# Two decoder layers in fp32 on one core: more 2x2 blocks with seven products in the feed-forward, and masked decay logs on ScalarE

## The chip, the core and the metric

The kernel runs on one core of a Trainium2 chip. The metric is the device time of one execution in microseconds (us), the median of several runs. Engines are named as the profile names them: PE is TensorE (PEld its weight loads), DVE VectorE, ACT ScalarE, POOL GpSimd, SP SyncE, whose queue issues the weight transfers.

## What is computed

Two layers over 256 tokens of width 2048, everything in fp32. Cut to what matters here:

```python
h = rms_norm(x, norm_mix_w[l])
proj = h @ w_in                                   # 2048 x about 6360 columns
y = concat([retention(...), mamba2(...), rwkv7(...)])
x = x + y @ w_out[l]
h = rms_norm(x, norm_ffn_w[l])
x = x + (silu(h @ ffn_w_gate[l]) * (h @ ffn_w_up[l])) @ ffn_w_down[l]   # D_FF = 5632
# in mamba2, for each of 16 heads and each chunk of 128 tokens:
a_cum = cumsum(dt * A); seg = a_cum[:, None] - a_cum[None, :]
decay_in = exp(where(causal, seg, -inf))          # 128 x 128 a head and chunk
```

## The kernel before

**One product in three passes.** Each fp32 operand is split into two fp32r tiles, high and low (x = xh + xl, w = wh + wl), and a product is xh·wh + xl·wh + xh·wl: three matmuls into one PSUM bank. 256 tokens are two row tiles (t = 0, 1) of 128. The weights are split on the chip: `fetch` has SP load raw tiles of 128x1024 (512 KB, five buffers `raw`), `split` lets ACT write `wh` (a copy to fp32r) and DVE `wl` (raw minus wh), with three buffers each. `plan` writes down the whole sequence of weight tiles ("parts"); `wtile` hands out the next part and emits the split of the one after it. The tiles' framework reorders instructions from this order by priority, but each engine then works through a fixed list.

**Gate and up.** `gate_up` makes 512 columns of gate and 512 of up at once (11 groups f a layer). Its inner dimension runs over eight pairs kp of two k-tiles. A pair is a product of 2x2 blocks: rows t, inner k, columns n (gate or up). Plain pairs take 8 block products, that is 24 matmuls. Pairs in `SEVEN` take 7 (21 matmuls) by a Winograd-like scheme: four PSUM banks C (`dn`) take what belongs to one output alone, four banks M (`mx`) what several share. Such a pair needs sums of weight blocks made on the chip: from two raw tiles DVE makes u1 (128x1024) and u2 (two ops of 128x512), then three tiles are split instead of two, and half a tile b besides. The parts are called s0, s1, s2. The sums of x blocks (`comb`) are made once a layer in `post_pair`, on POOL. After the last such pair ACT and DVE make z, w and y out of the banks M, and at the end of the group they add the banks C, take silu and multiply. `finish` (queued in `self.late`, run in the next group) transposes the result for the down projection and splits it.

**Down.** D_FF is done in two parts of 6 and 5 groups. For each of four column groups g `dense` multiplies over 12 or 10 pairs with two PSUM banks, 12 matmuls a raw tile, and `add_res` adds them to the residual `res`. Of four banks `dn` two are in use at a time. After the last part `post_x` transposes the new residual for the next layer.

**Mixers.** While the input projection runs in `dense`, generators in lanes (`queue`, `pump`) slip the mixers' small steps between its matmuls. `ssm_dt` has `masked` make the causal decay logs: for 8 heads at once, tril times a (high and low part apart), 128x1024 by one POOL op. There are 16 such ops in all, 8 a layer. Two matmuls with `triu_r` sum them, ACT takes exp. Not far from there in time, `rwkv`'s group norm runs on DVE as TENSOR_SCALAR of 128x64 a head (L113).

Of the kernel before, what the change touches and what calls it, by code (L numbers as in the profile page):

```python
# [23 lines left out]

FFN_PARTS = [6, 5]

SEVEN = (2, 5)

# [29 lines left out]
class Trunk:  # L58
# [194 lines left out]
    def plan(self):  # L253
        seq, parts, done = [], [], []

        def plain(tiles, kind="n"):
            for t in tiles:
                parts.append((kind, len(seq)))
                seq.append(t)
                done.append(len(seq))  # L260
        for l in range(DEPTH):
            off = 0
            for n in (IN_W[name] for name in IN_ORDER):
                plain((f"win{l}", off + kp * 2 * P * n, n) for kp in range(8))
                off += D * n
            for g in range(4):
                plain(("wout", (l * 4 + g) * D * 512 + kp * 2 * P * 512, 512) for kp in range(8))
            f0 = 0
            for nf in FFN_PARTS:
                for f in range(f0, f0 + nf):  # L270
                    for kp in range(8):
                        t = [("wgu", ((l * 11 + f) * 16 + 2 * kp + j) * P * 1024, 512) for j in range(2)]
                        if kp in SEVEN:
                            parts += [(f"s{j}", len(seq)) for j in range(3)]
                            seq += t
                            done += [len(seq)] * 3
                        else:
                            plain(t, "c")
# [145 lines left out]
    def post_pair(self, kp, src, scale, xh, xl):  # L424

        fl = lambda t: t.rearrange("p a b -> p (a b)")
        ps = self.PS()
        for k in range(2):
            for t in range(2):
                self.tr(ps[:, k * 256 + t * P:k * 256 + (t + 1) * P], src(t, k), self.ident)  # L430
        w = self.U()
        for k in range(2):
            self.act(w[:, k * 256:(k + 1) * 256], ps[:, k * 256:(k + 1) * 256], AF.Copy, scale=scale(k))
        self.act(fl(xh), w[:, :512], AF.Copy)
        self.tt(fl(xl), w[:, :512], fl(xh).bitcast(F32), ALU.subtract)
        if kp in SEVEN:
            a11, a21, a12, a22, s1, s2, s3, q = [w[:, i * P:(i + 1) * P] for i in range(8)]
            self.tt(s1, a21, a22, ALU.subtract, eng="pool")
            self.tt(s2, s1, a11, ALU.subtract, eng="pool")
            self.tt(s3, a11, a21, ALU.subtract, eng="pool")  # L440
            self.tt(q, a12, s2, ALU.add, eng="pool")
            c = self.U(F32R)
            self.act(c[:, 0:512], w[:, 512:1024], AF.Copy)
            self.tt(c[:, 512:1024], w[:, 512:1024], c[:, 0:512].bitcast(F32), ALU.subtract)
            self.comb[kp] = c
# [549 lines left out]
    def ssm_dt(self, l, raw):  # L995
# [58 lines left out]
        tl = self.cst("tril").rearrange("p (o c) -> p o c", o=1).to_broadcast([P, 8, P])  # L1054
# [12 lines left out]
        y = M["y"] = [None, None]  # L1067
# [217 lines left out]
        self.finish_x()  # L1285
        self.yt = None

    def gate_up(self, rstd):

        mm = self.nc.tensor.matmul  # L1290

# [6 lines left out]
        for kp in range(8):  # L1298
            xk = [self.xs(2 * kp + j) for j in range(2)]
            A = lambda t, k: tuple(h[:, t * P:(t + 1) * P] for h in xk[k])  # L1300
            if kp not in SEVEN:
                for k in range(2):
                    w = self.wtile(("c",))
                    for t in range(2):
                        for n in range(2):
                            prod(C[2 * t + n], A(t, k), blk(w, n), kp == 0 and k == 0, kp == 7 and k == 1)
            else:
                cb = self.comb[kp]
                S1, S2, S3, Q = [(cb[:, i * P:(i + 1) * P], cb[:, 512 + i * P:512 + (i + 1) * P]) for i in range(4)]
                first, last = kp == SEVEN[0], kp == SEVEN[-1]  # L1310
# [12 lines left out]
            if kp == 0:  # L1323
                self.flush()
            if kp == SEVEN[-1]:
                t0, t1, sg = self.U(), self.U(), self.U()
                z, w_, y, v = t0[:, 0:512], t0[:, 512:1024], t1[:, 0:512], t1[:, 512:1024]
                c0, c1 = sg[:, 0:512], sg[:, 512:1024]
                self.act(v, M[0], AF.Copy)
                self.tt(z, v, M[3], ALU.add)  # L1330
                self.tt(w_, M[1], z, ALU.subtract)
                self.tt(y, M[2], z, ALU.add)
# [11 lines left out]
        def finish(t):  # L1344
# [3 lines left out]
            o, p4 = hh[:, :, t * P:(t + 1) * P], ps.rearrange("p (k c) -> p k c", k=4)  # L1348
            self.act(o, p4, AF.Copy)
            self.tt(hl[:, :, t * P:(t + 1) * P], p4, o.bitcast(F32), ALU.subtract)  # L1350
        self.late += [lambda: finish(0), lambda: finish(1)]
        return hh, hl

    def ffn(self, l):
        f0 = 0
        xt, rstd = self.xt, self.rstd
        for pi, nf in enumerate(FFN_PARTS):
            hts = [self.gate_up(rstd) for f in range(f0, f0 + nf)]
            lastp = pi == len(FFN_PARTS) - 1

            def xs(k):
# [4 lines left out]
            for g in range(4):
                kps = list(range(2 * f0, 2 * (f0 + nf)))
                if lastp and l + 1 == DEPTH:
                    if g == 0:
                        fw = self.final_weight()  # L1370
                    if g == 3:
                        return self.final(kps, xs, fw)
                ps = self.dense(512, kps, xs, False)
                self.add_res(g, ps)
                if lastp:
                    if l + 1 < DEPTH:
                        self.post_x(l + 1, g, "nmw")
                    else:
                        self.squares(g)
                        for t in range(2):  # L1380
                            r = self.res[g][:, t, :]
                            self.tt(r, r, fw(g), ALU.mult)
# [122 lines left out]
def _layout(i):  # L1505
# [65 lines left out]

# [20 lines left out]
```

## Time and profile before

| | |
|---|---|
| median of 3 runs | 2423.09 us (2422.21 to 2423.18) |
| profiled execution | 2423.65 us, its span 2421.6 us |
| mean granted PE clock | 0.996 |
| HBM read | 430.66 MB, 179 GB/s over the span |

The span runs from the first instruction to the last; the time has some 2 us around it. Busy times and shares count one engine over the span. A group's line names the helper that records it: L103 is any DVE `tt`, L106 any POOL one, L121 any `act`, L307 and L308 the halves of a weight tile, L1294 a product in `gate_up`, L390 to L392 one in `dense`. In the tables by stretch, a column gives busy us and, in brackets, how many instructions.

### The profile page before, as it was taken

The page shows a single profiled execution, that of the slowest core. Times are in us where ns is not written, and L with a number is a line of the kernel's source. Part 1 is how long each engine was busy: PE and PEld are TensorE (multiplying, and loading weights), DVE is VectorE, ACT ScalarE, POOL GpSimd, SP SyncE. Part 2 cuts the span into 40 slices and gives each one's busy share as a digit, 9 for nine tenths or more (in the row PEclk, how much of TensorE's full clock was granted, in tenths as well). Part 3 has the DMA queues.
Part 4 walks back from the last instruction along what each step waited for, and adds up shares of the span by engine and source line. Part 5 has one row for each costly group of instructions (what it writes and reads, how often), then busy time and mean ns, then how long its engine had stood idle before and what let it go on. Part 6 is the DMA issues. An engine that isn't in the chain of part 4 may idle for free. (4 is left out here: it accounts for less than half of the span.)

```text
span 2421.6 us, 33651 instructions
## 1 busy us (share of the span) xinstructions
PE 2389.3 (99%) x13076; PEld 2023.5 (84%) x13076; DVE 1675.4 (69%) x2106; ACT 1206.7 (50%) x1506; POOL 152.1 (6%) x157
## 2 busy tenths in 40 slices
PE   8999899999999999999999999999999999999998
PEld 8998788888888878888899988887888888888886
DVE  7777756577886467876558876565878754688754
ACT  6445545555554345554454546455555543455543
POOL 2100320000000000000001113200000000000000
PEclk9999999999999999999999999999999999999999
DMA  8454345556555555565544544445555655555654
GB/s 290 147 170 115 133 154 174 179 184 202 192 197 190 189 188 194 187 213 191 184 164 143 165 122 153 157 165 182 192 195 188 200 191 191 184 197 196 215 187 144
DMA packets 139424, 436.01 MB, mean 180 GB/s; under 512 B 30464, under 2 KB 30720, under 8 KB 139264
## 3 DMA queue, kind: packets, MB, share of 16 engines
q1 hardware_dynamic: 137360, 428.52, 53.4%
q0 software_dynamic: 1184, 4.19, 0.5%
q8 instruction: 102, 1.67, 0.3%
q10 hardware_dynamic: 720, 1.15, 0.1%
q14 instruction: 58, 0.48, 0.1%
HBM read 430.66 MB, written 3.15 MB: 179 GB/s over the span
## 5 line engine op out<-in xcount | busy, mean ns | idle before, releaser
L308 DVE TENSOR_TENSOR wl<-raw,wh 128x1024 fp32r<-128x1024 f32 (+3 forms) x763 | 928.0, 1218 | 494.2 <-ACT wh L307 487.2
L307 ACT ACTIVATE wh<-raw 128x1024 fp32r<-128x1024 f32 (+3 forms) x763 | 793.8, 1042 | 893.1 <-PE dn L391 443.4
L1294 PE MATMUL dn<-wh,xh 128*128 128x512 f32 x1100 | 431.4, 392 | 2.3 <-DVE res L103 2.3
L1294 PE MATMUL dn<-wl,xh 128*128 128x512 f32 x1100 | 428.6, 390 | 0.0
L1294 PE MATMUL dn<-wh,xl 128*128 128x512 f32 x1100 | 428.5, 390 | 0.0
L391 PE MATMUL dn<-wh,u 128*128 128x512 f32 x920 | 363.4, 395 | 0.0
L390 PE MATMUL dn<-wh,u 128*128 128x512 f32 x920 | 363.0, 395 | 0.0
L392 PE MATMUL dn<-wl,u 128*128 128x512 f32 x920 | 362.1, 394 | 0.3 <-DVE wl L308 0.2
L382 PE MATMUL dn<-xh,wh 128*128 128x256 f32 x896 | 258.8, 289 | 7.8 <-ACT wh L307 7.8
L384 PE MATMUL dn<-xh,wl 128*128 128x256 f32 x896 | 254.8, 286 | 1.1 <-DVE wl L308 1.1
L383 PE MATMUL dn<-xl,wh 128*128 128x256 f32 x896 | 255.1, 285 | 0.0
L1294 PEld LDWEIGHTS dn<-wh,xh 128*128 128x128 f32 x1100 | 206.5, 188 | 48.9 <-DVE u L103 3.9
L1294 PEld LDWEIGHTS dn<-wl,xh 128*128 128x128 f32 x1100 | 206.4, 188 | 43.4
L1294 PEld LDWEIGHTS dn<-wh,xl 128*128 128x128 f32 x1100 | 206.6, 188 | 42.1
L390 PEld LDWEIGHTS dn<-wh,u 128*128 128x128 f32 x920 | 172.8, 188 | 40.3 <-DVE u L103 0.8
L392 PEld LDWEIGHTS dn<-wl,u 128*128 128x128 f32 x920 | 172.9, 188 | 39.8 <-DVE wl L308 1.1
L391 PEld LDWEIGHTS dn<-wh,u 128*128 128x128 f32 x920 | 172.8, 188 | 38.7
L382 PEld LDWEIGHTS dn<-xh,wh 128*128 128x128 f32 x896 | 173.7, 194 | 10.5 <-ACT wh L307 8.2
L392 PE MATMUL dn<-wl,xh 128*128 128x512 f32 (+2 forms) x448 | 164.3, 368 | 11.0 <-DVE wl L308 11.0
L384 PEld LDWEIGHTS dn<-xh,wl 128*128 128x128 f32 x896 | 173.1, 194 | 1.8 <-DVE wl L308 1.5
L383 PEld LDWEIGHTS dn<-xl,wh 128*128 128x128 f32 x896 | 173.9, 194 | 0.2
L390 PE MATMUL dn<-wh,xh 128*128 128x512 f32 (+2 forms) x448 | 170.9, 382 | 0.0
(177 smaller groups left out, 2725.6 us busy)
## 6 DMA issues: line engine op xcount, KB each, us to landing
raw<-wgu SPq DMA_DIRECT2D x352, 512.0 KB, 3.8
raw<-wdown SPq DMA_DIRECT2D x176, 512.0 KB, 4.2
raw<-win SPq DMA_DIRECT2D x175, 512.0 KB, 3.5
raw<-wout SPq DMA_DIRECT2D x64, 512.0 KB, 3.3
raw<-win SPq DMA_DIRECT2D x32, 340.0 KB, 2.9
raw<-win SPq DMA_DIRECT2D x16, 360.0 KB, 3.0
u<-xt SPq DMA_DIRECT2D x8, 256.0 KB, 7.2
res<-x SPq DMA_DIRECT2D x4, 512.0 KB, 5.2
```

Source lines behind the costliest of these rows:

```text
L307: nc.scalar.activation(wh[:, c], raw[:, c], AF.Copy)
L308: nc.vector.tensor_tensor(wl[:, c], raw[:, c], wh[:, c].bitcast(F32), op=ALU.subtract)
L382: nc.tensor.matmul(o, lhsT=wh[:, c], rhs=xh, start=st and m % 2 == 0, stop=False)
L383: nc.tensor.matmul(o, lhsT=wh[:, c], rhs=xl, start=False, stop=False)
L384: nc.tensor.matmul(o, lhsT=wl[:, c], rhs=xh, start=False, stop=sp and m % 2 == 1)
L390: nc.tensor.matmul(o, lhsT=xh[:, x], rhs=wh[:, c], start=st, stop=False)
L391: nc.tensor.matmul(o, lhsT=xl[:, x], rhs=wh[:, c], start=False, stop=False)
L392: nc.tensor.matmul(o, lhsT=xh[:, x], rhs=wl[:, c], start=False, stop=sp)
L1294: mm(o, lhsT=x[a], rhs=w[b], start=start and i == 0, stop=stop and i == 2)
```

## The change

1. `SEVEN` goes from two pairs to three of eight: kp = 2, 4, 5. Pairs 4 and 5 follow each other.
2. The inner loop of `gate_up` becomes `blocks`, and the down projection uses it too (`down`): two column groups at once as the two block columns, with seven products in pairs 2, 5, 8, 14, 17 and 19 of 22. The weights lie accordingly in `wdp`. The last two column groups of the last part of layer 2 stay in `dense` and `final`. So 21 pairs of the down projection have seven products: 6 in each of the first three of the parts, 3 in the last.
3. The sums of blocks of the hidden activations (`hcomb`) that this needs are made in `finish`, on DVE (`block_sums`), for one pair in six of the eleven groups of a layer.
4. `masked` makes its logs head by head on ACT, copy with a scale per partition: 128x128 each, 64 a layer in the place of 8 POOL ops.

Both versions compute the same function. The diff, without the layout of the weights on the host:

```diff
-SEVEN = (2, 5)
+SEVEN = (2, 4, 5)
+DOWN_SEVEN = (2, 5, 8, 14, 17, 19)
...
-                for g in range(4):
-                    plain(("wdown", (l * 4 + g) * D_FF * 512 + kp * 2 * P * 512, 512)
-                          for kp in range(2 * f0, 2 * (f0 + nf)))
+                    pairs("wgu", (l * 11 + f) * 16, range(8), SEVEN)
+                lastp = f0 + nf == 11
+                for g2 in range(2):
+                    if lastp and l + 1 == DEPTH and g2:
+                        for g in range(2):
+                            plain(("wdown", g * 2 * nf * 2 * P * 512 + kp * 2 * P * 512, 512) for kp in range(2 * nf))
+                    else:
+                        pairs("wdp", (l * 2 + g2) * 44, range(2 * f0, 2 * (f0 + nf)), DOWN_SEVEN)
...
+    def block_sums(self, w, eng):
+        eng = None if eng == "dve" else eng
+        a11, a21, a12, a22, s1, s2, s3, q = [w[:, i * P:(i + 1) * P] for i in range(8)]
+        self.tt(s1, a21, a22, ALU.subtract, eng=eng)
+        self.tt(s2, s1, a11, ALU.subtract, eng=eng)
+        self.tt(s3, a11, a21, ALU.subtract, eng=eng)
+        self.tt(q, a12, s2, ALU.add, eng=eng)
+        c = self.U(F32R)
+        self.act(c[:, 0:512], w[:, 512:1024], AF.Copy)
+        self.tt(c[:, 512:1024], w[:, 512:1024], c[:, 0:512].bitcast(F32), ALU.subtract)
+        return c
...
         def masked(i):
             r = []
             for ap in (ah.bitcast(F32), al):
                 m = self.U(F32R)
-                self.tt(m[:, :1024].rearrange("p (h c) -> p h c", h=8), tl,
-                        ap[:, 8 * i:8 * i + 8].rearrange("p (h o) -> p h o", o=1).to_broadcast([P, 8, P]),
-                        ALU.mult, eng="pool")
+                for h in range(8):
+                    self.act(m[:, h * P:(h + 1) * P], tl, AF.Copy, scale=ap[:, 8 * i + h:8 * i + h + 1])
+                    if h % 4 == 3:
+                        yield 1
                 r.append(m)
-                yield 2
...
-    def gate_up(self, rstd):
+    def blocks(self, kps, xs, comb, mid):
...
-            if kp == SEVEN[-1]:
-                t0, t1, sg = self.U(), self.U(), self.U()
...
+                if last:
+                    mid(M)
...
+            for b in need:
+                self.act(need[b][:, 0:512].rearrange("p (k s c) -> p k s c", k=2, s=2)[:, :, t, :],
+                         p4[:, 2 * b:2 * b + 2, :], AF.Copy)
+                if t:
+                    self.hcomb[2 * f + b] = self.block_sums(need[b], "dve")
+        need = {b: self.U() for b in range(2) if 2 * f + b in DOWN_SEVEN}
         self.late += [lambda: finish(0), lambda: finish(1)]
...
+    def down(self, g2, kps, xs):
+        t0, t1 = self.U(), self.U()
+        z, w, y, v = t0[:, 0:512], t0[:, 512:1024], t1[:, 0:512], t1[:, 512:1024]
+        r = [self.res[2 * g2 + n][:, t, :] for t in range(2) for n in range(2)]
+        def mid(M):
+            self.sums_of(M, v, z, w, y)
+            self.tt(r[0], r[0], v, ALU.add)
+            self.tt(v, M[1], y, ALU.subtract)
+            for a, b in ((1, w), (2, y), (3, v)):
+                self.tt(r[a], r[a], b, ALU.add)
+        C, _ = self.blocks(kps, xs, self.hcomb, mid)
+        for a in range(4):
+            self.tt(r[a], r[a], C[a], ALU.add)
```

Here is how the fixed lists change at three places. First DVE in the third gate and up group of layer 1, from the second split of pair 3 on. In the list before come the splits of pair 4 and then pair 5; `wl` is a half of a weight tile, L329 is u1, L331 and L332 are u2, L336 is b:

```order
L308 TENSOR_TENSOR wl_5778<-raw_5664,wh_5777 128x1024
L308 TENSOR_TENSOR wl_5796<-raw_5696,wh_5795 128x1024
L329 TENSOR_TENSOR u_5831<-raw_5724,raw_5769 128x1024
L331 TENSOR_TENSOR u_5832<-u_5831,raw_5724 128x512
L308 TENSOR_TENSOR wl_5814<-raw_5722,wh_5813 128x1024
L332 TENSOR_TENSOR u_5832<-u_5832,raw_5769 128x512
L336 TENSOR_TENSOR u_5840<-raw_5769,u_5840 128x512
L308 TENSOR_TENSOR wl_5837<-raw_5724,wh_5836 128x1024
L308 TENSOR_TENSOR wl_5860<-u_5831,wh_5859 128x1024
L308 TENSOR_TENSOR wl_5873<-u_5832,wh_5872 128x1024
```

In the changed list (L317 is the half of a tile there, L338, L340, L341 and L345 the sums), DVE at the same place:

```order
L317 TENSOR_TENSOR wl_5872<-raw_5749,wh_5871 128x1024
L338 TENSOR_TENSOR u_5889<-raw_5790,raw_5816 128x1024
L317 TENSOR_TENSOR wl_5895<-raw_5790,wh_5894 128x1024
L340 TENSOR_TENSOR u_5890<-u_5889,raw_5790 128x512
L317 TENSOR_TENSOR wl_5918<-u_5889,wh_5917 128x1024
L341 TENSOR_TENSOR u_5890<-u_5890,raw_5816 128x512
L345 TENSOR_TENSOR u_5898<-raw_5816,u_5898 128x512
L338 TENSOR_TENSOR u_5940<-raw_5818,raw_5863 128x1024
L317 TENSOR_TENSOR wl_5931<-u_5890,wh_5930 128x1024
L340 TENSOR_TENSOR u_5941<-u_5940,raw_5818 128x512
L317 TENSOR_TENSOR wl_5946<-raw_5818,wh_5945 128x1024
L341 TENSOR_TENSOR u_5941<-u_5941,raw_5863 128x512
```

Two runs of sums now interlock, with no plain pair between them.

Second, POOL in the mixers of layer 1, from the rsqrt of `rwkv`'s group norm on (a power of 128x8). Before, six masks (`u<-cc,ah` and `u<-cc,s`, 128x1024) come behind it:

```order
L106 TENSOR_TENSOR s_3164<-s_3164,negh 128x8
L106 TENSOR_TENSOR u_3234<-cc,ah_2981 128x1024
L106 TENSOR_TENSOR u_3269<-cc,s_2983 128x1024
L106 TENSOR_TENSOR u_3310<-cc,ah_2981 128x1024
L106 TENSOR_TENSOR u_3334<-cc,s_2983 128x1024
L106 TENSOR_TENSOR u_3450<-cc,ah_2981 128x1024
L106 TENSOR_TENSOR u_3470<-cc,s_2983 128x1024
L106 TENSOR_TENSOR u_3560<-u_3542,cc 128x4x64 x2
```

Now POOL goes from the power to the rotary ops of retention:

```order
L108 TENSOR_TENSOR u_3156<-u_3078,s_3036 128x1024
L108 TENSOR_TENSOR s_3164<-s_3164,negh 128x8
L108 TENSOR_TENSOR u_3597<-u_3579,cc 128x4x64 x4
L108 TENSOR_TENSOR u_3811<-u_3793,cc 128x4x64 x4
L108 TENSOR_TENSOR u_2359<-u_2359,u_3873 128x512
```

Third, ACT at the same time, in the last columns z of the input projection (weight tiles of 128x680). Before:

```order
L307 ACTIVATE wh_3257<-raw_3110 128x680
L307 ACTIVATE wh_3278<-raw_3148 128x680
L121 ACTIVATE u_3242<-mx_3243,pp_79 128x256 x2
L121 ACTIVATE u_3242<-mx_3250,pp_79 128x256 x2
L307 ACTIVATE wh_3298<-raw_3175 128x680
L307 ACTIVATE wh_3322<-raw_3193 128x680
L121 ACTIVATE u_3318<-u_3242 128x1024
L307 ACTIVATE wh_3342<-raw_3226 128x1024
```

And changed, with the masks (`u<-cc,ah` and `u<-cc,s`, 128x128) between the weight tiles:

```order
L316 ACTIVATE wh_3260<-raw_3110 128x680
L123 ACTIVATE u_3234<-cc,ah_2981 128x128 x4
L316 ACTIVATE wh_3283<-raw_3148 128x680
L123 ACTIVATE u_3245<-mx_3246,pp_79 128x256 x2
L123 ACTIVATE u_3245<-mx_3253,pp_79 128x256 x2
L123 ACTIVATE u_3295<-cc,s_2983 128x128 x4
L316 ACTIVATE wh_3307<-raw_3175 128x680
L123 ACTIVATE u_3295<-cc,s_2983 128x128 x4
L123 ACTIVATE u_3329<-u_3245 128x1024
L316 ACTIVATE wh_3333<-raw_3193 128x680
```

The weight tiles of the input projection now stand behind four masks each in ACT's list.

More of the change, by code (lines that the diff above doesn't have):

```diff
@@ L260, in plain, with pairs @@
                 done.append(len(seq))
+        def pairs(w, first, kps, seven):
+            for kp in kps:
+                t = [(w, (first + 2 * kp + j) * P * 1024, 512) for j in range(2)]
+                if kp in seven:
+                    parts.extend((f"s{j}", len(seq)) for j in range(3))
+                    seq.extend(t)
+                    done.extend([len(seq)] * 3)
+                else:
+                    plain(t, "c")
         for l in range(DEPTH):
@@ L270, in plan @@
                 for f in range(f0, f0 + nf):
[L271 to L278, printed above, removed]
-                for g in range(4):
-                    plain(("wdown", (l * 4 + g) * D_FF * 512 + kp * 2 * P * 512, 512)
-                          for kp in range(2 * f0, 2 * (f0 + nf)))
+                    pairs("wgu", (l * 11 + f) * 16, range(8), SEVEN)
[4 more added lines that the diff above has]
+                            plain(("wdown", g * 2 * nf * 2 * P * 512 + kp * 2 * P * 512, 512) for kp in range(2 * nf))
+                    else:
+                        pairs("wdp", (l * 2 + g2) * 44, range(2 * f0, 2 * (f0 + nf)), DOWN_SEVEN)
                 f0 += nf
@@ L436, in post_pair @@
         if kp in SEVEN:
[L437 to L445, printed above, removed]
+            self.comb[kp] = self.block_sums(w, "pool")
+    def block_sums(self, w, eng):
[9 more added lines that the diff above has]
+        return c
     def squares(self, g):
@@ L1297, in gate_up @@
         blk = lambda w, j: tuple(t[:, j * 512:(j + 1) * 512] for t in w)
-        for kp in range(8):
-            xk = [self.xs(2 * kp + j) for j in range(2)]
+        seven = [kp for kp in kps if kp in comb]
+        for kp in kps:
+            xk = [xs(2 * kp + j) for j in range(2)]
             A = lambda t, k: tuple(h[:, t * P:(t + 1) * P] for h in xk[k])
-            if kp not in SEVEN:
+            if kp not in seven:
                 for k in range(2):
@@ L1305, in gate_up @@
                         for n in range(2):
-                            prod(C[2 * t + n], A(t, k), blk(w, n), kp == 0 and k == 0, kp == 7 and k == 1)
+                            prod(C[2 * t + n], A(t, k), blk(w, n), kp == kps[0] and k == 0, kp == kps[-1] and k == 1)
             else:
-                cb = self.comb[kp]
+                cb = comb[kp]
                 S1, S2, S3, Q = [(cb[:, i * P:(i + 1) * P], cb[:, 512 + i * P:512 + (i + 1) * P]) for i in range(4)]
-                first, last = kp == SEVEN[0], kp == SEVEN[-1]
+                first, last = kp == seven[0], kp == seven[-1]
                 if first:
@@ L1357, in ffn @@
         for pi, nf in enumerate(FFN_PARTS):
-            hts = [self.gate_up(rstd) for f in range(f0, f0 + nf)]
+            self.hcomb = {}
+            hts = [self.gate_up(f, rstd) for f in range(f0, f0 + nf)]
             lastp = pi == len(FFN_PARTS) - 1
@@ L1365, in ffn, with mid, last_group @@
                 self.new_x()
[L1366 to L1376, printed above, removed]
-                        self.post_x(l + 1, g, "nmw")
[L1378 to L1382, printed above, removed]
-            f0 += nf
+            kps = list(range(2 * f0, 2 * (f0 + nf)))
+            for g2 in range(2):
+                last = lastp and l + 1 == DEPTH
+                if last and g2:
+                    ps = self.dense(512, kps, xs, False)
+                    self.add_res(2, ps)
+                    self.last_group(2, fw)
+                    return self.final(kps, xs, fw)
+                if last:
+                    fw = self.final_weight()
+                self.down(g2, kps, xs)
+                for g in (2 * g2, 2 * g2 + 1):
+                    if last:
+                        self.last_group(g, fw)
+                    elif lastp:
+                        self.post_x(l + 1, g, "nmw")
+            f0 += nf
+    def down(self, g2, kps, xs):
+        t0, t1 = self.U(), self.U()
+        z, w, y, v = t0[:, 0:512], t0[:, 512:1024], t1[:, 0:512], t1[:, 512:1024]
+        r = [self.res[2 * g2 + n][:, t, :] for t in range(2) for n in range(2)]
+        def mid(M):
+            self.sums_of(M, v, z, w, y)
[6 more added lines that the diff above has]
+            self.tt(r[a], r[a], C[a], ALU.add)
+    def last_group(self, g, fw):
+        self.squares(g)
+        for t in range(2):
+            r = self.res[g][:, t, :]
+            self.tt(r, r, fw(g), ALU.mult)
     def final_weight(self):
@@ L1488, in _tiles, with _pairs @@
     return np.ascontiguousarray(w.reshape(k, 2, P, n).transpose(0, 2, 1, 3)).reshape(-1)
-def _pairs(a, b):
+def _pairs(a, b, seven):
     k = a.shape[0] // (2 * P)
@@ L1496, in _pairs @@
     for kp in range(k):
-        if kp in SEVEN:
+        if kp in seven:
             o[kp, 0, :, 0], o[kp, 0, :, 1], o[kp, 1, :, 0], o[kp, 1, :, 1] = \
```

33 lines of the change are left out of this document (21 added, 12 removed).

## The prediction

> **What bounds the kernel now.** I read the engine shares on the page first, then what PE waited for, then stretches of the feed-forward.
>
> ```profile
> PE 2389.3 (99%) x13076; PEld 2023.5 (84%) x13076; DVE 1675.4 (69%) x2106; ACT 1206.7 (50%) x1506; POOL 152.1 (6%) x157
> ```
>
> In the list of waits (total us, times, longest), the first three of PE are:
>
> ```profile
> PE dn L392 <- DVE wl L308: 11.2, 5, 6.0
> PE dn L382 <- ACT wh L307: 7.8, 3, 6.0
> PE dn L1294 <- DVE res L103: 2.3, 2, 1.5
> ```
>
> PE hardly waits: 21.3 us in these three, of which the 7.8 fall in the first 250 us and stay. The time is the number of matmuls times their distance, plus a few stalls. The busy 0.39 us of a row overlaps its neighbours; the price of a matmul is the distance of starts. In PE's timeline these two rows of gate and up are 24 matmuls apart, and so are the two of the down projection:
>
> ```profile
> 523.03 0.39 PE L1294 MATMUL dn<-wh,xl 128*128 128x512 f32 x1
> ...
> 528.47 0.39 PE L1294 MATMUL dn<-wh,xl 128*128 128x512 f32 x1
> ```
> ```profile
> 789.84 0.40 PE L390 MATMUL dn<-wh,u 128*128 128x512 f32 x1
> ...
> 795.41 0.39 PE L390 MATMUL dn<-wh,u 128*128 128x512 f32 x1
> ```
>
> That is 5.44/24 = 0.227 us and 5.57/24 = 0.232 us. Three gate and up groups by stretch (us, then PE, PEld, DVE, ACT, POOL busy, clock, DMA share, GB/s):
>
> ```profile
> 531.50:574.30 42.80, 42.80 (x193) 35.21 (x192) 34.41 (x39) 22.60 (x25) 0.00 (x0) 1.00 0.58 193
> ...
> sum 128.60, PE 128.60 PEld 105.78 DVE 103.30 ACT 68.19 POOL 0.00; mean PE 42.87 PEld 35.26 DVE 34.43 ACT 22.73 POOL 0.00
> ```
>
> PE is full, and DVE is the next engine, at 34.4 of 42.9 us. That is what the change loads further.
>
> **Products.** A seven-product pair has 21 matmuls instead of 24. Gate and up: 22 groups x 3 = 66, x 0.227 = 15.0 us. Down: 21 pairs x 3 = 63, x 0.232 = 14.6 us. All lie on the bounding engine: **-29.6 us**.
>
> **Masks.** Where POOL makes masks, DVE stands still. POOL, DVE and PE in their timelines:
>
> ```profile
> 260.52 1.89 POOL L106 TENSOR_TENSOR u<-cc,ah 128x1024 fp32r<-128x1024 f32 x1
> ...
> 269.78 2.52 POOL L106 TENSOR_TENSOR u<-cc,s 128x1024 fp32r<-128x1024 f32 x1
> ```
> ```profile
> 260.58 7.44 DVE L113 TENSOR_SCALAR u<-u,s,s 128x64 f32<-128x64 f32 x4 [1.75 <-POOL s L106]
> 267.94 2.60 DVE L308 TENSOR_TENSOR wl<-raw,wh 128x680 fp32r<-128x680 f32 x1
> 270.47 2.55 DVE L113 TENSOR_SCALAR u<-u,s,s 128x64 f32<-128x64 f32 x4
> 278.39 0.87 DVE L308 TENSOR_TENSOR wl<-raw,wh 128x680 fp32r<-128x680 f32 x1 [0.51 <-ACT wh L307]
> ```
> ```profile
> 270.60 0.65 PE L392 MATMUL dn<-wl,xh 128*128 128x340 f32 x1 [6.02 <-DVE wl L308]
> ```
>
> Four tiny group-norm ops take 7.44 us, one POOL mask each, and the half of a weight tile behind them 2.60 us instead of 0.87. PE waits 6.0 us, and then its granted clock is down:
>
> ```profile
> 265.00:270.00 5.00, 0.00 (x0) 0.00 (x0) 5.00 (x3) 0.00 (x0) 5.00 (x4) 0.93 0.00 0
> 270.00:275.00 5.00, 4.40 (x17) 4.35 (x18) 5.00 (x8) 1.08 (x2) 2.30 (x1) 0.50 0.28 85
> 275.00:280.00 5.00, 5.00 (x31) 5.00 (x30) 3.18 (x4) 2.97 (x6) 0.00 (x0) 0.89 0.81 295
> ```
>
> At half clock for 4.4 us and 0.89 for 5 us PE loses 2.2 + 0.5 = 2.7 us more. PE's waits at the masks further on in layer 1, and in layer 2, with one stretch there:
>
> ```profile
> PE dn L392 <- DVE wl L308: 1.2, 1, 1.2
> ...
> PE dn L392 <- DVE wl L308: 3.8, 2, 2.5
> ```
> ```profile
> 1480.00:1485.00 5.00, 2.61 (x15) 2.09 (x14) 5.00 (x6) 4.49 (x7) 3.41 (x2) 1.00 0.04 16
> ```
>
> Together 6.0 + 2.7 + 1.2 + 3.8 = 13.7 us hang on these ops. They leave POOL, so DVE is free there. SBUF — State Buffer in the Trainium skill ("Who interferes with whom") says that DVE and GpSimd take one shared port pair for a whole instruction, and that ScalarE never waits for it; the 1.86 us that each blocked op takes agree, and by that rule alone the whole 13.7 us would come back and the sum below be 2 us lower.
>
> What comes instead is load on ACT. A copy with a scale per partition of 128x128 isn't in the trace; two rows bracket it:
>
> ```profile
> L121 ACT ACTIVATE s<-dn,s 128x16 f32<-128x16 f32 x4 | 1.1, 275 | 0.8 <-PE dn L392 0.8
> L121 ACT ACTIVATE u<-dn,s 128x340 f32<-128x340 f32 x8 | 4.3, 540 | 2.3 <-PE dn L392 2.3
> ```
>
> Between them, 128 columns are 275 + 112/324 x 265 = 367 ns, so 64 are at most 23 us a layer, in some 60 us of the input projection. ACT is 50% busy over the span, so on the whole it fits. At one spot in each layer it crowds: from one 128x680 tile to the next ACT now has four masks and four 128x256 copies, some 3 us, while PE uses up such a tile in about 1.8 (12 x 0.227 x 340/512) and has two in hand. I give back 1 us a layer. The ends are nothing gained (ACT is late by as much as DVE was) and 13.7; I take the near end because the blocked rows are many times their free length: **-11.7 us**.
>
> **Ends of groups.** The 2.3 us of PE on `res` are the two turns from `dense` to gate and up, where two banks close only at the end. In `down` the first bank closes 9 matmuls (2 us) before the end and its add takes 0.7, so they go. Against that, `post_x` of two column groups now comes at once at the end of layer 1, 8 pieces of 128x256 on DVE behind four adds: between 0 and 5 us, what these pieces take (8 x 0.6, bounded by a 128x512 op); I take 2, since the next projection starts with other columns. **-0.3 us.**
>
> **DVE in gate and up.** Prices, by line and form, and the true distance of DVE's starts:
>
> ```profile
> L308 DVE TENSOR_TENSOR wl<-raw,wh 128x1024 fp32r<-128x1024 f32 x713 | 875.5, 1230 | 477.2 <-ACT wh L307 470.5
> L329 DVE TENSOR_TENSOR u<-raw,raw 128x1024 f32<-128x1024 f32 x44 | 53.6, 1219 | 11.8 <-DMA raw<-wgu 11.6
> L331 DVE TENSOR_TENSOR u<-u,raw 128x512 f32<-128x512 f32 x44 | 30.4, 691 | 1.4
> L103 DVE TENSOR_TENSOR u<-u,u 128x128 f32<-128x128 f32 x4 | 1.1, 284 | 0.0
> ```
> ```profile
> 747.27 1.22 DVE L308 TENSOR_TENSOR wl<-raw,wh 128x1024 fp32r<-128x1024 f32 x1
> 748.41 0.68 DVE L103 TENSOR_TENSOR u<-u,dn 128x512 f32<-128x512 f32 x1
> 749.00 0.68 DVE L103 TENSOR_TENSOR u<-mx,u 128x512 f32<-128x512 f32 x1
> ```
>
> So 1.14 us for 128x1024 and 0.6 for 128x512. A plain pair costs DVE 2 x 1.14 = 2.3 us against 5.4 of PE; a seven-product pair 4 x 1.14 + 3 x 0.6 + 0.1 = 6.5 us against 21 x 0.227 = 4.8. A group goes from 34.4 to 38.6 us, and with block sums for the down projection (4 x 0.28 + 0.6 = 1.7) to 40.3, of 42.2 us of PE. On average it holds; in the burst of pairs 4 and 5 it doesn't, and DVE lives on its lead. The lead before, at a group's turn:
>
> ```profile
> 531.64 0.39 PE L1294 MATMUL dn<-wh,xh 128*128 128x512 f32 x1
> ```
> ```profile
> 529.80 0.69 DVE L103 TENSOR_TENSOR u<-u,dn 128x512 f32<-128x512 f32 x1 [1.31 <-PE dn L1294]
> ...
> 540.63 1.21 DVE L329 TENSOR_TENSOR u<-raw,raw 128x1024 f32<-128x1024 f32 x1
> ```
>
> From the group's first matmul (0), DVE reaches u1 of pair 2 at 9.0 us; PE reaches pair 2 at 48 x 0.227 + 0.7 (the rest of 42.87, transposes) = 11.6, then pairs 3, 4, 5, 6 at 16.3, 21.8, 26.5, 31.3. With four small sums ahead u1 starts at 10.1. Going down the changed list with 1.14 and 0.6: u1 of pair 2 done 11.4, half for s1 13.7, b 14.9, s2 16.0, pair 3 at 17.2 and 18.3; pair 4: u1 19.4, s0 20.6, s1 22.3, b 23.5; pair 5: u1 24.7, (s2 of 4) 25.8, s0 27.6, b 28.8, s1 29.9, s2 31.1; pair 6 32.2. PE's list needs b of pair 2 at its 15th matmul, 14.7 (0.2 late), and in pair 5 s0 at 27.7, b at 28.8, s1 at 29.7, s2 at 30.8, pair 6 at 32.0 (0.3 late). So 0.5 us in the 12 groups with block sums; in the other 10 DVE is 1.7 us earlier and nothing waits: **+6 us**. The ends: 0, since PE has no wait here to win back; and 22 us, 1 us a group, because the slack is gone and each of DVE's waits for raw tiles (the 11.6 us in the L329 row, 7 times, 1.7 us each) would now reach PE.
>
> **At nothing:** the sums' ACT part (24 pieces of about 0.4 us, 12 of 0.6), under an ACT that is busy 22.7 of 42.9 us; 8 more small POOL sums in the output projection, needed only in pair 4 of the next group; the 22 `u` buffers, which the sixth group of a part just fills (3 `comb`, 10 activations, 3 `hcomb`, 3 for the output, 3 for a pair), as DVE frees a pair's three in the order in which the next asks for them; the transfers (the same bytes; if late, it is the 1.7 us above).
>
> **Sum**, against the profiled execution: 2423.65 - 29.6 - 11.7 - 0.3 + 6 = 2388.05 us. The median of the runs is 0.56 lower, so I forecast **2388 us**.
>
> **Rivals.**
> - *DVE pays for it.* The lead doesn't build up, every group waits about 1 us at pairs 5 and 6: 22 instead of 6, 2404 us. For it: no slack in the walk above; against: DVE's 2 to 4 us of idle time left in a group.
> - *The masks only move the stall.* ACT's weight halves come late by what DVE's did: 2388 + 11.7 = 2400 us. For it: the crowding above; against: ACT's free half.
> - *Slower.* The same late DVE, but as a long wait: the two pairs' 13 us against 9.7 of PE show 3.3 us where no lead is left. It decides at 41.6/22 = 1.9 us a group; at 2.5 us the time is 2423.65 - 41.6 + 55 = 2437. Above some length the clock falls too: after 6.0 us it did, after 2.5 us (clock 1.00 in 1480 to 1485) not. TensorE: Matmul & The Clock Gate ("What's actually happening") in the Trainium skill puts that at one idle window of some 3.4 us; both rows agree, and by that a whole 3.3 us would sit just at the edge. With 2.7 us more a group it would be near 2500.
> - *No change to speak of:* the products go, and all of the above goes wrong in part, to within 0.2% of 2423 (4.8 us, about what a measurement can tell from no change).
>
> **Chances.** My sum 0.68, with 2377 (13.7 and 2.3 won, no DVE waits) to 2399; DVE pays 0.16, 2399 to 2416; masks move the stall 0.09, 2396 to 2408; slower 0.04; no change 0.03. All but the last two are faster by over 0.2%: 0.93. The range 2377 to 2406 leaves out some 2 in 10, most of them above.
>
> **What would show it.** The same distances of starts and 129 fewer matmuls; no DVE op of 128x64 beyond 0.5 us in the mixers, no PE wait of 6 us and a clock of 1.00 from 250 to 300 us; PE waits on `wl`, b or u of under 1 us in gate and up, at pairs 2, 5 and 6; DVE busy 90 to 96% there. I am wrong if those waits come in every group at over 1 us, if ACT's `wh` is what PE waits for in the mixers, or if the clock dips in the feed-forward.

## Result and the profile after

The changed kernel takes 2400.5 us (median of four, 2398.7 to 2405.2), the kernel before 2422.7 on the same chip: ratio 0.9915, 95% interval 0.9897 to 0.9932. That is 22 us (0.85%) faster, where 35 were forecast (2388 us). The profiled execution is one of 2401.8 us, with a span of 2400.0 against 2421.6. The page, and the first of PE's waits:

```profile
PE 2374.5 (99%) x12947; PEld 1994.1 (83%) x12947; DVE 1874.1 (78%) x2439; ACT 1312.9 (55%) x1761; POOL 119.8 (5%) x149
```
```profile
PE dn L391 <- ACT wh L316: 7.4, 2, 6.3
PE mx L131 <- DVE u L113: 1.7, 2, 1.3
PE mx L1309 <- DVE wl L317: 1.5, 3, 0.7
```

129 matmuls are gone, of the 11.2 us for `wl` 1.1 are left (L401, further down the list), and the 2.3 for `res` have left the list. The 7.4 us are those of the first 250 us (7.8 before). The last line is all that the list has for gate and up: 0.9 of its 1.5 us lie there, in the first groups of the two layers, and 0.6 in a down projection. So where is the rest? By the starts of the first product and of the last one in each run of gate and up groups:

| stretch | before, us | after | change | forecast |
|---|---|---|---|---|
| start to gate and up of layer 1 | 488.3 | 481.7 | -6.6 | -8.9 |
| gate and up, 22 groups | 953.5 | 952.2 | -1.3 | -11.3 |
| down, first parts | 269.6 | 260.4 | -9.2 | -8.4 |
| down, second part of layer 1, to gate and up of layer 2 | 589.0 | 586.4 | -2.6 | -5.0 |
| last down and end | 121.2 | 119.3 | -1.9 | -2.1 |

(The forecast's terms are put where they were to act: products by their matmuls, masks in rows 1 and 4 with 1 us given back in each, the `res` waits and the 6 us of DVE in row 2, `post_x` in row 4.) 10 of the 14 us that are missing lie in gate and up. Two groups there by stretch, without and with block sums for the down projection:

```profile
524.82:567.54 42.72, 42.72 (x192) 35.10 (x191) 38.51 (x44) 24.41 (x27) 0.00 (x0) 1.00 0.60 199
611.38:655.20 43.82, 43.71 (x193) 34.79 (x191) 39.88 (x49) 25.24 (x30) 0.00 (x0) 1.00 0.60 193
```

The first is 0.65 us shorter than before (43.37), which is about three matmuls (0.68): as forecast. The second is 1.1 us longer than the first, and PE is still "busy" for 43.71 of its 43.82 us. The lost time shows only in the distances of starts. These are rows of the second group, at its pair 2 (the last two at its pair 5):

```profile
620.90 1.02 DVE L105 TENSOR_TENSOR u<-u 128x128 f32<-128x128 f32 x4 [0.45 <-ACT u L123]
621.84 1.22 DVE L338 TENSOR_TENSOR u<-raw,raw 128x1024 f32<-128x1024 f32 x1
622.97 0.69 DVE L105 TENSOR_TENSOR u<-u,u 128x512 fp32r<-128x512 f32 x1
623.17 1.06 ACT L316 ACTIVATE wh<-u 128x1024 fp32r<-128x1024 f32 x1 [0.58 <-DVE u L338]
624.14 0.61 ACT L344 ACTIVATE u<-raw 128x512 fp32r<-128x512 f32 x1
624.38 0.39 PE L1309 MATMUL dn<-wl,u 128*128 128x512 f32 x1
624.80 0.50 PE L1309 MATMUL dn<-u,xh 128*128 128x512 f32 x1
625.14 0.39 PE L1309 MATMUL dn<-u,xl 128*128 128x512 f32 x1
625.41 0.69 DVE L341 TENSOR_TENSOR u<-u,raw 128x512 f32<-128x512 f32 x1
626.21 1.06 ACT L316 ACTIVATE wh<-u 128x1024 fp32r<-128x1024 f32 x1 [1.46 <-DVE u L341]
626.75 0.50 PE L1309 MATMUL dn<-u,xh 128*128 128x512 f32 x1
627.32 0.50 PE L1309 MATMUL mx<-wh,u 128*128 128x512 f32 x1
...
640.73 0.60 ACT L123 ACTIVATE u<-mx 128x512 f32<-128x512 f32 x1 [1.36 <-PE mx L1309]
641.23 1.05 ACT L316 ACTIVATE wh<-u 128x1024 fp32r<-128x1024 f32 x1
```

Four small sums, then u1, then the low half of the small sums' split (L105, 128x512) on DVE; ACT's half of u1 waits for u1, and ACT's copy for b (L344) stands behind that half in ACT's list though it needs only the raw tile. PE asks for b at the pair's 7th matmul and starts it at 624.80, 0.42 us after its neighbour and not 0.23; at 627.32 the 16th matmul starts 0.57 us behind, just after ACT has ended s2's half (626.21 + 1.06 = 627.27), which had waited 1.46 us for DVE's second half of u2 (L341). A third such spot is s2 of pair 5 (a distance of 0.41, at 642.33): ACT's half of it (641.23) stands behind the copy of a bank M (640.73), which waits for PE. Behind each, the next distance is 0.34 and not 0.23: a restart costs 0.11 us more. Waits of 0.19, 0.34 and 0.18 plus 3 x 0.11 make 1.04 of the 1.10 us, and all 12 groups with block sums repeat it at the same three matmuls (42.7 against 43.8): 13 us. The idle column can't show it, since a row of 0.39 at a distance of 0.23 covers the first 0.16 us of any wait (one of 0.50, as before 627.32, 0.27). Perfetto Trace Analysis in the Trainium skill ("Identifying the Most-Contended Engine") calls the busy share of matmuls a poor measure because they are pipelined, and points to that of the weight loads; here PEld falls from 35.10 to 34.79 us in a longer stretch, which agrees.

The mixers, in the stretches shown before:

```profile
265.00:270.00 5.00, 5.00 (x36) 4.98 (x35) 2.86 (x3) 5.00 (x15) 0.00 (x0) 1.00 0.75 242
270.00:275.00 5.00, 4.92 (x33) 4.64 (x32) 4.27 (x6) 5.00 (x12) 0.00 (x0) 1.00 0.51 168
275.00:280.00 5.00, 5.00 (x25) 4.33 (x26) 2.20 (x2) 5.00 (x15) 0.00 (x0) 1.00 0.69 211
...
1480.00:1485.00 5.00, 5.00 (x23) 4.09 (x23) 4.65 (x5) 4.83 (x12) 0.00 (x0) 1.00 0.67 201
```
```profile
L123 ACT ACTIVATE u<-cc,ah 128x128 fp32r<-128x128 f32 x64 | 20.5, 396 | 0.0
L123 ACT ACTIVATE u<-cc,s 128x128 fp32r<-128x128 f32 x64 | 20.2, 400 | 0.0
L115 DVE TENSOR_SCALAR u<-u,s,s 128x64 f32<-128x64 f32 x32 | 7.6, 309 | 6.6 <-POOL s L108 6.6
```

ACT is now full (5.00 of 5.00) where PE stood still, PE is busy, the clock is 1.00, and the 128x64 ops of the group norm take 0.31 us each.

### The profile page after: what moved, and what is told of

The parts are those of the page before. It is cut to its first block, busy times and chain, and to the rows that moved or that the text cites. A ratio compares the mean times of both kernels' runs of the same rounds, so it can differ in the third digit from the quotient of the medians.

```text
span 2400.0 us, 34089 instructions
## 1 busy us (share of the span) xinstructions
PE 2374.5 (99%) x12947; PEld 1994.1 (83%) x12947; DVE 1874.1 (78%) x2439; ACT 1312.9 (55%) x1761; POOL 119.8 (5%) x149
## 4 chain that ended last, share of the span: by engine, by line
PE 87%; DVE 6%; ACT 3%; DMA 2%; issue 2%; POOL 0%; ACTq 0%; SPq 0%; POOLq 0%; DVEq 0%
PE dn L1309 41%; PE mx L1309 9%; PE dn L401 6%; PE dn L399 6%; PE dn L400 6%; PE dn L391 4%; PE dn L393 4%; PE dn L392 4%; PE mx L131 4%; DVE wl L317 2%; ACT wh L316 2%; PE mx L135 2%; DVE u L105 2%; ACT u L123 1%; DVE u L338 1%
## 5 line engine op out<-in xcount | busy, mean ns | idle before, releaser
L317 DVE TENSOR_TENSOR wl<-raw,wh 128x1024 fp32r<-128x1024 f32 (+3 forms) x720 | 866.3, 1211 | 284.5 <-ACT wh L316 277.9
L1309 PE MATMUL dn<-wh,xh 128*128 128x512 f32 x946 | 372.0, 393 | 0.0
L1309 PE MATMUL dn<-wh,xl 128*128 128x512 f32 x946 | 368.9, 390 | 0.0
L1309 PE MATMUL dn<-wl,xh 128*128 128x512 f32 x946 | 365.0, 390 | 0.0
L1309 PE MATMUL dn<-wh,u 128*128 128x512 f32 x1128 | 352.4, 394 | 0.0
L316 ACT ACTIVATE wh<-u 128x1024 fp32r<-128x1024 f32 x174 | 184.7, 1062 | 215.2 <-PE dn L1309 100.3
L317 DVE TENSOR_TENSOR wl<-u,wh 128x1024 fp32r<-128x1024 f32 x174 | 211.5, 1222 | 53.9 <-ACT wh L316 53.8
L1309 PEld LDWEIGHTS dn<-wh,u 128*128 128x128 f32 x1128 | 211.1, 188 | 48.1 <-DVE u L105 0.8
L1309 PE MATMUL dn<-wl,u 128*128 128x512 f32 x564 | 220.8, 394 | 0.1
L1309 PE MATMUL mx<-wh,u 128*128 128x512 f32 x564 | 180.8, 398 | 0.9
L401 PE MATMUL dn<-wl,xh 128*128 128x512 f32 (+2 forms) x448 | 162.4, 366 | 1.2 <-DVE wl L317 1.1
```

Source lines behind the costliest of these rows:

```text
L316: nc.scalar.activation(wh[:, c], raw[:, c], AF.Copy)
L317: nc.vector.tensor_tensor(wl[:, c], raw[:, c], wh[:, c].bitcast(F32), op=ALU.subtract)
L401: nc.tensor.matmul(o, lhsT=xh[:, x], rhs=wl[:, c], start=False, stop=sp)
L1309: mm(o, lhsT=x[a], rhs=w[b], start=start and i == 0, stop=stop and i == 2)
```

## Experiments

Three theories for the 13 us of gate and up: **A (place):** DVE's and ACT's lists are worked in order, and the small sums stand ahead of work that PE needs sooner. **B (load):** DVE has too much to do in such a group, wherever it stands. **C (burst):** two seven-product pairs in a row (4, 5) are too much. Each kernel was timed in five rounds against the kernel before on its chip; the changed kernel's ratio of 0.9915 is what the others compare with.

**1. The block sums late.**

```diff
         self.late = []
+        self.late6 = []
...
             if kp == kps[0]:
                 self.flush()
+            if kp == kps[6]:
+                for p, w in self.late6:
+                    self.hcomb[p] = self.block_sums(w, "dve")
+                self.late6 = []
...
                 if t:
-                    self.hcomb[2 * f + b] = self.block_sums(need[b], "dve")
+                    self.late6.append((2 * f + b, need[b]))
```

> The changed kernel, with one thing moved: the four block sums of the activations (and their split) that the down projection needs are made behind pair 6 of the next gate and up group, where DVE has 2 us free, instead of ahead of its pair 2. Theory A (place): in the changed kernel these sums push DVE's first sum of pair 2 back by 1 us, ACT's halves queue up behind it, and PE has three short stalls (0.19, 0.34 and 0.18 us, and 0.11 us more each until it runs at its distance again), 1.1 us in each of 12 groups. All 13 us go: about 2387.5 us, all groups at 42.7 us. Theory B (load): DVE has too much work in such a group wherever it stands, and the stalls only move: 2398 to 2402 us, no change. Theory C (burst): the stalls at pair 2 go, the one in pair 5 comes from two seven-product pairs in a row and stays: 12 x 0.28 = 3.4 us less won, 2391 us.

Measured: 2386.0 us, ratio 0.9852 (0.9838 to 0.9865), and the groups with sums take 42.73 to 42.79 us. The same group by stretch, and DVE and ACT at its pair 2:

```profile
608.79:651.54 42.75, 42.75 (x192) 35.05 (x191) 39.62 (x49) 25.71 (x30) 0.00 (x0) 1.00 0.60 198
```
```profile
617.78 1.22 DVE L339 TENSOR_TENSOR u<-raw,raw 128x1024 f32<-128x1024 f32 x1
618.91 0.28 DVE L105 TENSOR_TENSOR u<-u 128x128 f32<-128x128 f32 x1
619.11 1.06 ACT L317 ACTIVATE wh<-u 128x1024 fp32r<-128x1024 f32 x1 [0.83 <-DVE u L339]
619.12 0.69 DVE L341 TENSOR_TENSOR u<-u,raw 128x512 f32<-128x512 f32 x1
619.72 0.28 DVE L105 TENSOR_TENSOR u<-u 128x128 f32<-128x128 f32 x1
```

u1 starts 8.99 us into the group instead of 10.46. DVE's busy time is the same (39.62 against 39.88), its 49 instructions too, and all of the 13 us are back (14.1 us in gate and up; 15.3 in all by the two ratios): theory A, and B falls. DVE's list isn't the code's order: two of the four sums stand ahead of the halves of u2, where they take 0.4 us, the others behind pair 6's first split, and the sums' own split further on. Other entries moved with them: DVE has both halves of u2 ahead of the next half of a weight tile, and ACT has s2's half of pair 5 ahead of the copy of the bank M. So the place in the lists is the cause, but what each of these moves is worth was not parted.

**2. The sums on POOL, at the old place.** Edit: `self.block_sums(need[b], "pool")`.

> The changed kernel with the four block sums for the down projection on POOL instead of DVE, at the same place in the code. If only DVE's order counts (theory A) and POOL works beside DVE: DVE is free of them, the stalls go, 2387 to 2390 us. If DVE and POOL exclude each other, as in the rows of the masks before: a sum of 128x128 takes POOL 0.73 us against DVE's 0.21, so DVE can lose up to 2.9 us where it lost 1.0, and the stalls grow by up to 1.9 us in each of 12 groups: 2400 to 2423 us. By theory B (load) POOL without exclusion would win back about half, 2394 us.

Measured: 2412.9 us, ratio 0.9962 (0.9949 to 0.9974); the 12 groups take 44.70 to 44.79. The time lies in the range that exclusion was to give (2400 to 2423 us), but the rows of the same group show another cause:

```profile
620.34 1.22 DVE L338 TENSOR_TENSOR u<-raw,raw 128x1024 f32<-128x1024 f32 x1
620.92 2.33 POOL L108 TENSOR_TENSOR u<-u 128x128 f32<-128x128 f32 x4 [42.42 <-ACT u L123]
623.28 0.63 ACT L123 ACTIVATE u<-u 128x512 fp32r<-128x512 f32 x1 [2.44 <-POOL u L108]
623.95 0.69 DVE L105 TENSOR_TENSOR u<-u,u 128x512 fp32r<-128x512 f32 x1 [2.39 <-ACT u L123]
624.56 0.69 DVE L340 TENSOR_TENSOR u<-u,raw 128x512 f32<-128x512 f32 x1
625.43 0.50 PE L1309 MATMUL dn<-u,xh 128*128 128x512 f32 x1 [0.69 <-ACT u L344]
```

u1 starts on time. Then DVE stands idle for 2.39 us: the next entry of its list is the low half of the split, which waits for POOL's four sums and ACT's copy. u2 (L340), which could run, is behind it. That is a wait in order, not contention.

**3. Late, and on POOL**, which parts the two (the edit of 1 with `"pool"`).

> The version with the late block sums, and these four sums on POOL, so that DVE has 1.1 us less in each of the 12 groups. In the run with the sums on POOL at their old place, groups took 2.05 us more than 42.72, and DVE stood 2.4 us idle there: the low half of the split stands between DVE's first and second sum of pair 2 in its list, and waits for POOL's four sums (2.3 us) and ACT's copy behind them. Theory W (DVE waits in order): with the split late, nothing waits for POOL, all groups take 42.7 us, 2386 us, as with the late sums on DVE. Theory L (DVE and POOL exclude each other for whole instructions, as at the masks): DVE loses 2.3 us where it had 1.1 us of sums, and late in the group it has 2 us free, so up to 0.5 us a group comes through: 2386 to 2392 us, and DVE ops of 1.22 us that run beside POOL's sums show up to 0.7 us more.

Measured: 2396.6 us, ratio 0.9903 (0.9888 to 0.9917), groups of 43.38 to 43.47, 0.7 us over 42.72. Nothing waits for POOL's result, yet:

```profile
619.26 4.09 POOL L108 TENSOR_TENSOR u<-u 128x128 f32<-128x128 f32 x4 [39.33 <-ACT u L123]
619.93 0.83 DVE L341 TENSOR_TENSOR u<-u,raw 128x512 f32<-128x512 f32 x1
621.55 1.48 DVE L318 TENSOR_TENSOR wl<-u,wh 128x1024 fp32r<-128x1024 f32 x1
622.96 0.95 DVE L346 TENSOR_TENSOR u<-raw,u 128x512 fp32r<-128x512 f32 x1
```

Beside DVE, POOL's sums take 4.09 us for four instead of 2.33, and four DVE ops 0.14 to 0.27 us more each (0.83 for 0.69, 1.48 for 1.22): 0.8 us together up to the end of b's low half (L346), for which PE then waits (a distance of 0.78). I expected these sums late in the group; they started as data came in, at pair 2. So the two engines do hold each other up, and it costs 0.7 us a group here, less than the 2 us of the wait in order. The time is above both forecasts (2386 and up to 2392 us): against experiment 1 the profiled execution loses 8.5 us in gate and up, and 6.5 between the feed-forwards, where its clock was at 0.5 for 13.7 us (see the end). SBUF — State Buffer in the Trainium skill ("Who interferes with whom") calls the port pair that DVE and GpSimd share an exclusive lock; these rows show both stretched, by parts of an instruction.

**4. Only the split late** (sums stay in `finish`, `block_split` is called at pair 6).

> The changed kernel with the four sums on DVE at their place, and only their split (ACT's copy of 128x512 and DVE's difference of 128x512) moved late into the group. This parts the two pieces of theory A. The first sum of pair 2 is still 0.6 to 0.9 us late, so the wait for the pair's b (0.19 + 0.11 us) stays at least in part; the difference of 0.6 us between the first and the second sum goes, so s2 of pair 2 (0.34 + 0.11) and of pair 5 (0.18 + 0.11) come in time. If both pieces count by their length: 8 to 13 of the 13 us go, 2387 to 2392 us. If it is the four sums alone that matter: 2398 to 2401 us.

Measured: 2387.3 us, ratio 0.9862 (0.9846 to 0.9879), groups of 42.69 to 42.76. It doesn't part what it was to part: with the split gone the list changed here too, u1 starts at 8.98, three sums follow behind it and the fourth between the halves of u2. It shows that 0.8 us of sums behind u1 cost nothing when the split is late.

**5. No seven-product pairs in the down projection:** `DOWN_SEVEN = ()`.

> The changed kernel without the seven-product pairs of the down projection: no block sums for them in the gate and up groups, and 63 matmuls more. Third pair of gate and up and masks stay. Theory A (place): +63 x 0.232 = 14.6 us of products, -13 us of stalls in the 12 groups: about 2402 us, all groups at 42.7 us. Theory C (burst of pairs 4 and 5): one stall of 0.28 us stays per group or in these 12, 2405 us. If the third pair itself overloads DVE in every group (the forecast's rival): the stalls stay, 2413 to 2416 us.

Measured: 2401.4 us, ratio 0.9915 (0.9901 to 0.9928). All groups but the first of each part take 42.72 to 42.84 us, with the third pair of gate and up in them. Pairs 4 and 5 in a row cost nothing by themselves in these groups: C falls, and the changed kernel spent on stalls nearly all that the down projection's products had won. Against experiment 1 the down products are worth 15.3 us (0.9915 - 0.9852).

**6. Pairs spread:** `SEVEN = (2, 4, 6)`.

> The changed kernel with the seven-product pairs of gate and up spread: 2, 4 and 6 instead of 2, 4 and 5; the block sums for the down projection stay where the change has them. Theory A (place): the two stalls at pair 2 in the 12 groups stay (0.75 us each group together), the one in pair 5 goes with ACT's copy of the first M bank, which moves behind pair 6: 3.4 us less, 2397 us, if nothing new waits at the group's end, where the M banks now close 5 us later. Theory C (the burst of pairs 4 and 5 as the main cause): the larger part of the 13 us goes, 2390 us. If the end of the group gets crowded (first sums behind pair 6 and the next group's first tile late), 22 groups lose up to 1 us: 2400 to 2415 us.

Measured: 2406.1 us, ratio 0.9931 (0.9918 to 0.9943). The stalls at pair 2 stay and the one in pair 5 is gone, as A has it (43.5 us in most of the 12 groups), but A's 2397 us don't come: the other groups grew to 42.9 to 43.4, and the first of each layer most (45.88 and 46.68):

```profile
481.89:527.77 45.88, 43.62 (x192) 34.77 (x191) 36.55 (x43) 27.03 (x35) 6.87 (x5) 1.00 0.54 177
614.48:657.96 43.48, 43.39 (x192) 34.95 (x191) 40.12 (x49) 25.48 (x30) 0.00 (x0) 1.00 0.61 193
```

In the first one PE is idle for 2.3 us. Its longest wait (a distance of 1.64 us) is for a `wl` that stands in DVE's list behind a u1, and this u1 waits 2.93 us for a raw tile; experiment 7 comes back to that. Why the other groups grew was not followed; the spread is worse than the burst.

**7. The third pair undone in the kernel of experiment 1:** `SEVEN = (2, 5)`.

> The version with the block sums late, without the third seven-product pair of gate and up (2 and 5, as before the change): 66 matmuls more and 2.1 us less of DVE in each group. If no stall hangs on the third pair any more: +66 x 0.227 = 15.0 us, 2401 us. If the third pair still costs PE hidden waits, less: 2394 to 2400 us.

Measured: 2402.9 us, ratio 0.9915 (0.9901 to 0.9929): 15.3 us against experiment 1, the 66 matmuls. The first groups of the layers take 43.29 and 43.31 us, as all others do; where there are three pairs, they take up to 1.7 us more than the others (44.48 against 42.75 in experiment 4). Two rows of DVE in the first group of layer 2 of the changed kernel show why:

```profile
1688.38 1.23 DVE L338 TENSOR_TENSOR u<-raw,raw 128x1024 f32<-128x1024 f32 x1 [2.75 <-DMA raw<-wgu]
1689.52 1.22 DVE L317 TENSOR_TENSOR wl<-u,wh 128x1024 fp32r<-128x1024 f32 x1
```

u1 of pair 4 waits 2.75 us for a raw tile, and the low half of pair 2's s2 stands behind it; PE starts that tile's `mx<-wl,u` at 1690.80, 0.87 us late. The loss goes with this wait: with 1.86 us of it the first group takes 42.78 us (experiment 1, layer 1), with 2.19 and 2.75 us 43.13 and 43.71 (the changed kernel), with 3.49 us 44.48 (experiment 4, layer 2).

**8. The masks back on POOL in the changed kernel** (`masked` as it was).

> The changed kernel with the masked decay logs back on POOL, two broadcast products of 128x1024 for each half, as before the change; products as in the changed kernel. As on record, the masks' term is 11.7 us: 2412 us. By the segments of the two traces (start to the first gate and up group 6.6 us shorter; in layer 2 the waits at the masks 4.1 us shorter, but 3 us of new waits and a cold clock in place): 2407 to 2410 us, with the 6 us wait of PE and a half clock back in 250 to 300 us, and the clock dip at 1435 us gone if it hangs on the masks. If the masks only moved the stall: 2400 us.

Measured: 2414.3 us, ratio 0.9968 (0.9956 to 0.998), 12.8 us by the ratios. PE's 6 us wait in layer 1 is back, and in layer 2 there is one of 4.6 us with a cold clock (below 1.00) behind it, where the kernel before had one of 2.65 and a clock of 1.00:

```profile
PE dn L401 <- DVE wl L317: 12.8, 6, 6.0
```
```profile
1470.00:1475.00 5.00, 0.85 (x3) 0.86 (x4) 5.00 (x7) 0.07 (x1) 3.37 (x2) 0.78 0.00 0
1475.00:1480.00 5.00, 5.00 (x21) 5.00 (x20) 2.98 (x4) 1.06 (x1) 0.00 (x0) 0.54 0.88 270
```

**9. The masks alone**, on the kernel before.

> The kernel before with one part of the change alone: the masked decay logs head by head on ScalarE; products as before. By the term on record (11.7 us, which the run with the masks back on POOL supports): 2421.9 - 11.7 = 2410 us, no PE wait of 6 us and no 2.65 us wait at the masks of layer 2. In the changed kernel layer 2 has a PE wait of 1.3 us for a small DVE op at the start of the group norms and a cold clock right behind it; the run with the masks on POOL has that wait too, so it should come with the products' other order of DVE and not stand here. If it comes with the masks, it stands here too and the gain is 8 to 9 us: 2413 us.

Measured: 2411.9 us, ratio 0.9951 (0.9937 to 0.9964), 11.9 us. 8.0 of them lie ahead of gate and up of layer 1, 4.2 between the feed-forwards. PE's longest wait for a small DVE op in the mixers of layer 2 is 0.75 us over its distance, as before (0.73); in the changed kernel and in all versions with new products it is 1.4, with the third pair alone (experiment 5) and with the down products alone (7) too. So it comes with the products; by which change of the lists, I did not test.

**10. One more down pair in the kernel of experiment 1:** `DOWN_SEVEN = (2, 5, 8, 13, 15, 17, 19)`.

> The version with the block sums late, with one more seven-product pair in the second part of the down projection (13, 15, 17 and 19 instead of 14, 17 and 19): 3 x 3 = 9 matmuls less, 9 x 0.232 = 2.1 us, if the late sums fit into four groups of each second part as they do into three: 2384 us. If DVE or the raw tiles can't keep up in the down projection (PE waited 0.6 us for a wl at its second seven-product pair): 2386 us or more.

Measured: 2385.8 us, ratio 0.9846 (0.9832 to 0.9859). The groups behind the first of each part take 42.6 to 42.8, so the fourth set of sums fits, but 2 us are below what the intervals tell apart. The versions of experiments 1, 4 and 10 are faster than both kernels.

## Why the prediction was right in its direction and short in its size

The time of 2400.5 us lies in the range (2377 to 2406), but 1.5 us above the end of the range for the sum itself (2399), in that of the rival in which DVE pays (2399 to 2416). What failed is the sum's DVE term. It failed by late work, as that rival has it, but on ACT as well as on DVE, in 12 groups and not in 22, and at pairs 2 and 5 and not at 5 and 6.

- **Products, -29.6:** right. The distances of starts held (medians of 0.227 in gate and up and 0.231 in down, before and after), and experiments 5 and 7 put down and gate and up at 15.3 us each (forecast 14.6 and 15.0).
- **Masks, -11.7:** right as a sum: 11.9 alone, 12.8 taken back. Two parts of it were off and cancelled. The wait of 1.2 us further on in layer 1 stayed (1.3 over the distance, with the masks alone too): the `wl` it is for stands in DVE's list behind an op that waits 2.03 us for POOL's rotary products, which are still there. And the 1 us a layer given back to a crowded ACT did not come: ACT is full there and PE does not wait for it. A mask of 128x128 takes ACT 398 ns, against the 367 that two rows gave. The rival that masks only move the stall is out.
- **Ends of groups, -0.3:** the `res` waits are gone, as forecast. `post_x` in pairs brings no wait of its own. The first groups of the layers are late instead (43.13 and 43.71 against 42.72), which they are only in versions with the third pair. This is a raw tile that comes late (experiment 7): the transfers stood at nothing in the sum, and here that gave away 1.4 us.
- **DVE in gate and up, +6:** this is the step that failed; it is 13. The 12 groups with block sums and the 10 without were told apart rightly, and the rival with 22 late groups is wrong. But the walk gave each 0.5 us where it is 1.1. It followed DVE alone: ACT's list was never walked, in which b's copy stands behind the half that waits for u1, s2's half waits for the end of u2, and in pair 5 stands behind the copy of a bank M. It set b against the pair's 15th matmul, which is where DVE's low half of it is needed (it ends at 626.70, the matmul starts at 626.75); but PE asks for ACT's high half at the 7th and for ACT's half of s2 at the 16th. And it had no price for the restart, 0.11 us a stall. "No slack in the walk" was the sign that a term of 0.5 us per group could not be trusted to 0.5.
- **What was to be seen:** waits at pairs 2 and 5 of under 1 us, DVE at 91%, the clock of 1.00 from 250 to 300 us: all there. But the list of waits shows none of the 13 us: its 1.5 us on `wl` lie in the first groups of the layers and in a down projection.
- **Not in the sum:** some 3 us between the feed-forwards: a wait of 0.8 us in the second down part of layer 1 (where DVE's u1 had waited for a raw tile), the wait of 1.4 instead of 0.7 in the mixers of layer 2, and a clock of 0.5 for 3.4 us behind that (below), at most 1.7 us in the profiled execution.

## What to carry to other kernels

When an engine that is nearly full gets small extra work, it is the place in its list that costs, not the length: 1.5 us of sums and split, ahead of and between the links of a chain from DVE over ACT to PE, cost 1.1 us a group here, and nothing where most of it came later. Walk the lists of all engines of the chain, not of the busiest alone, and add a restart for each stall. On a pipelined engine look for short waits in the distances of starts, or in the chain that ended last, not in busy shares: with PE at 99% in both, the chain gave DVE and ACT 9% in the changed kernel and 4% with the sums late.

```profile
PE 87%; DVE 6%; ACT 3%; DMA 2%; issue 2%; POOL 0%; ACTq 0%; SPq 0%; POOLq 0%; DVEq 0%
```
```profile
PE 94%; DVE 2%; ACT 2%; issue 1%; DMA 1%; POOL 0%; SPq 0%; POOLq 0%; DVEq 0%; ACTq 0%
```

## What the hardware showed beside

The clock falls after waits much shorter than the 6.0 us at the masks, and not each time. In layer 2 of the changed kernel PE waits 1.28 us, with matmuls of 32x32 around it; the late version has the same wait:

```profile
1430.00:1435.00 5.00, 3.72 (x45) 2.94 (x45) 4.60 (x16) 1.28 (x3) 0.00 (x0) 1.00 0.54 155
1435.00:1440.00 5.00, 5.00 (x34) 4.21 (x33) 3.10 (x5) 1.35 (x3) 2.80 (x2) 0.66 0.30 78
```
```profile
1420.00:1425.00 5.00, 3.72 (x46) 2.85 (x44) 4.60 (x16) 1.28 (x3) 0.00 (x0) 1.00 0.55 150
1425.00:1430.00 5.00, 5.00 (x55) 4.17 (x54) 4.55 (x6) 2.12 (x4) 4.20 (x2) 1.00 0.32 83
```

The first falls to a mean of 0.66 over its stretch (0.5 for 3.4 us), the second keeps 1.00. Of the ten profiled versions with this wait (1.23 to 1.29 us), the clock falls right behind it in four: for 3.4 us in the changed kernel and in experiment 4, for 13.7 us in experiments 3 and 10. Before the change the clock fell at one place without any wait to speak of, behind 16 matmuls of 8 columns:

```profile
1283.76 1.95 PE L129 MATMUL mx<-cc,u 128*128 128x8 f32 x16 [0.18 <-ACT u L121]
...
1285.00:1290.00 5.00, 5.00 (x31) 5.00 (x31) 1.33 (x2) 0.16 (x1) 3.89 (x2) 0.66 0.74 238
```

TensorE: Matmul & The Clock Gate in the Trainium skill ("What's actually happening") puts a fall at one idle window of some 3.4 us, and has that window run freely. These rows show falls with less idle time than that; that tiny matmuls count as idle, and that chance sets where the window lies, would fit them, and was not tested. It goes with a few microseconds: of the changed kernel's four timed executions the one of 2398.7 us has a mean clock of 0.999, and that of 2405.2 us 0.996.
